# Modulation rounds interleaved with an RWKV recurrence in program order

## The chip, the cores and the metric

The kernel runs on one core of one Trainium2 chip. The metric is the device time of one execution in microseconds (us). Before the change it is 2808.48 us, the median of 3 runs (2804.44 to 2815.34). Times below are counted from the start of the profiled span.

## The reference

Two transformer blocks of depth 2 run one after the other on 256 tokens of width 1024 (a context of 256 tokens goes with them). Layer 0 of the first block mixes tokens with an RWKV-7 recurrence and a Mamba scan; the other three layers are neighbourhood attention with experts, differential attention with a short convolution, and a Fourier mixer. Each of the four layers is steered by a *modulation*: six vectors of 1024 (shift, scale and gate, twice), computed from a conditioning vector alone:

```python
m_lat = jnp.split((c_lat_act @ w_ada[i] + b_ada[i])[:, None, :], 6, axis=-1)
a_lat = _modulate(_rms_norm(h_lat, norm_mix[i]), m_lat[0], m_lat[1])
...
def step(S, inp):
    r_t, w_t, k_t, v_t, a_t, b_t = inp
    sa = jnp.einsum('bhvk,bhk->bhv', S, a_t)
    S = S * w_t[:, :, None, :] + sa[..., None] * b_t[:, :, None, :] + v_t[..., None] * k_t[:, :, None, :]
    return S, jnp.einsum('bhvk,bhk->bhv', S, r_t)
```

Everything is in 32-bit floats. The weights of the four modulations are 4 x 1024 x 6144 numbers, some 100 MB.

## The kernel before

**The modulations in rounds.** Each layer's modulation is cut into 3 rounds, 12 in all (`ADA`). A round (`ada_round`, L360) reads 8 slices of 128 rows by 2048 columns, each as two loads of 512 KB into `raw` tiles on SyncE's queue (`ada_load`, L345 to L353), and issues 4 matmuls per slice (L377) into the one bank `ada`. The four write 32 partitions each. Then VectorE adds the bias into `adar` (L380), ScalarE's queue stores it to `mrows` (L383), TensorE transposes it into `adat` (L386), and VectorE copies the columns to `mcol` (L391). Five `raw` buffers serve the rounds here, and the layer weights before and after them. `filler(n)` (L396) advances the rounds by n pieces; a round has 10 pieces.

**The recurrence.** Round 0 is done before anything else. The other 11 rounds stand beside the recurrence (`rwkv`, L798), which handles 8 blocks (2 halves of the tokens, 2 sub-blocks, 2 groups of heads). For each block k, P prepares it (`lw`, `ic`, `ci`, `sc`, `et`, `bt` on TensorE; `rw_decay`, `rw_keys`, `rw_scores`), I inverts a 32x32 triangle in 31 dependent pairs of VectorE instructions (L1012, L1013), Q completes the inverse (`m`), and C runs the two chunk steps (`rw_step`, L1048): products into `Z`, copies to `zs` and `UV` on ScalarE and VectorE, products again, and the new state `YM` (L1095). The blocks' triangles go through device memory: `dsc` to `E` before the inverse (L765, L768) and `dx` to `EA` after it (L1018, L1022), half of each on SyncE's queue, between the loads of the rounds. F (`rw_finish`, L1105) normalises a finished half (L1114 to L1122), transposes it (`yT`), multiplies with the gate (`gt`) and writes `rkv` (L1144). The sequence of these parts is a written list:

```python
ORDER = 'P0 I0 P1 I1 Q0 C0 P2 I2 Q1 C1 P3 I3 Q2 C2 F0 P4 I4 Q3 C3 F1 P5 I5 Q4 C4 P6 I6 Q5 C5 P7 I7 Q6 C6 F2 Q7 C7 F3'
```

After F3, `rw_end` (L831) splits the mixer's output in two float32r parts, `oH` and `oL`. `mixer_out` (L1369) loads the residual rows `h` on ScalarE's queue (L506), and the output projection begins: its weights are split into `wh` on ScalarE (L203) and `wl` on VectorE (L204), and its products go to `xs` (L248 to L250).

**What sets the order.** The Tile framework orders each engine's instructions by simulating the program: of what is ready, the instruction with the highest priority goes first, and priority falls with the place in the program. In this kernel all 11 rounds stand in the program ahead of the recurrence, but with their priority lowered by 100000, so that anything of the recurrence that is ready goes first. On the chip each engine then runs its list strictly in that order.

Of the kernel before, what the change touches and what calls it, by code (L numbers as in the profile page):

```python
# [51 lines left out]
HOT = 0  # L52
WB = 1, 1
HOTM = 100000
APRI = -100000
NROW = 5
NU, ND, NM, NYM, NB, NR, NW, NMB = 8, 3, 4, 6, 2, 6, 4, 7
NFIRST = 3000
# [7 lines left out]
class Builder:  # L66
# [221 lines left out]
    def weave(s, *gens, fill=0):  # L288

        gens = [[g, n] for g, n in gens]  # L290
        while gens:
            for x in list(gens):
                for _ in range(x[1]):
                    if next(x[0], s_end) is s_end:
                        gens.remove(x)
                        break
                while fill and s.work >= fill:
                    s.work -= fill
                    s.filler(1)


    def pool(s, name, bufs, **kw):
# [348 lines left out]
    def in_proj(s, xH, xL):  # L651
        nc, I = s.nc, s.I
        W = I["mix_w_in"]
        z13, t0, t1 = s.misc
        s.tl = [t0, t1]

        def ev(j, p):
            if j == 0:
                z12 = s.row(nm="z12")
                s.shift_mix(12, p, z12)  # L660
                for d in range(2):
                    for o in (32, 96):
                        nc.gpsimd.memset(s.tl[d][o:o + 1, :], 1.0)
                    nc.scalar.activation(s.tl[d][0:32, :], z12[32 * d:32 * d + 32, :], AF.Tanh)
                    nc.vector.tensor_copy(s.tl[d][64:96, :], z12[64 + 32 * d:96 + 32 * d, :])
            else:
                s.shift_mix(13, p, z13)

                nc.scalar.activation(z13[0:96, :], z13[0:96, :], AF.Tanh, scale=0.5)
                nc.gpsimd.tensor_scalar(z13[0:96, :], z13[0:96, :], 0.5, 0.5, op0=ALU.mult, op1=ALU.add)  # L670
        s.run(s.wstat2(I["wi_misc"], xH, xL, ev))
        s.z13 = z13
        s.rkv = {}
        s.rw_init()

        def krv_proj(half):
            for nm, o in (("k", 512), ("r", 0), ("v", 1024)):
                if nm == "k":
                    for th in range(2):
                        s.KR[th, half] = s.unit(nm="KR").rearrange("p (x j t) -> p x j t", x=2, j=2)  # L680
                if nm == "v":
                    t = s.rkv["v", half] = s.mx.tile([128, 2, 512], F32, name=s.n("rkv"))
                    z = lambda j: t[:, j]
                else:
                    z = lambda j: [s.KR[th, half][:, int(nm == "r"), j] for th in range(2)]
                yield from s.wstat2(W[:, o + half * 256:o + half * 256 + 256], xH, xL,
                                    lambda j, p: s.shift_mix(o // 128 + half * 2 + j, p, z(j)))
                if nm == "k":
                    s.rw_kk(half)

        s.xbc = [s.unit(nm="xbc").rearrange("p (a t) -> p a t", a=2) for _ in range(4)]
        s.xbc = [x[:, a] for x in s.xbc for a in range(2)]
        s.dump("@xbc")
        for c in range(4):
            s.run(s.wstat2(W[:, 2272 + c * 256:2272 + c * 256 + 256], xH, xL,
                           lambda j, p: s.conv5(c * 2 + j, p, s.xbc[c * 2 + j])))

        s.zg = [s.unit(nm="zg").rearrange("p (a t) -> p a t", a=2) for _ in range(2)]
        s.zg = [x[:, a] for x in s.zg for a in range(2)]

        def z_proj():
            yield from s.xstat(W, slice(1760, 2272), xH, xL, range(4), lambda t, p: nc.scalar.activation(s.zg[t], p, AF.Silu))
        s.dump("@weave")
        s.weave((s.hot(s.mamba(), HOTM), WB[0]), (s.chain(krv_proj(0), z_proj(), krv_proj(1)), WB[1]))
        xH = xL = None
        s.wstop()
        s.dump("@ada")
        s.fill = ADA[1:NADA]
        with s.tc.high_priority(offset=APRI):
            s.filler(999)  # L710
        s.run(s.rwkv())
        s.dump("@s7")
        s.rw_end()

# [1645 lines left out]
```

## Time and profile before

| | |
|---|---|
| median of 3 runs | 2808.48 us |
| the profiled execution | 2815.26 us |
| its span (first to last instruction) | 2813.5 us |
| mean granted TensorE clock | 0.945 |
| the recurrence with its 11 rounds | about 246 to 688 us |
| busy shares | TensorE 93%, VectorE 67%, ScalarE 46%, GpSimd 6% |

The profile's "busy" is the union of an engine's instructions; TensorE's weight loads (PEld) are counted apart. An engine that waits at the head of its list shows as idle, with the instruction or transfer that ended the wait. The fp32 matmuls leave two records each, so the 4 matmuls of a slice are 8 records and a round is 64. The granted clock is a mean between 0.5 (1.2 GHz) and 1.0 (2.4 GHz).

### The profile page before, as it was taken

Reading aid. Unit: us, or ns where it says so; the run is one execution under the profiler, and the core shown is the slowest. Engines: PE = TensorE matmul, PEld = TensorE weight load, DVE = VectorE, ACT = ScalarE, POOL = GpSimd, SP = SyncE. Lnnn points to the kernel's source line nnn. Section 1 sums busy time; section 2 is a strip of 40 time slices with the busy share of each in tenths; the row PEclk is TensorE's granted clock in tenths of the full one; section 3 lists DMA queues with packets and bytes.
Section 4 is the critical chain, followed back from the end, with each engine's and each line's share of the span. In section 5 each row is a group of like instructions: output and inputs, shape, how many; then the busy total and the mean of one; then the engine's idle time right before and its main releaser. Section 6 shows DMA issues by size and latency. Waiting matters only on the chain. (4 is left out here: it accounts for less than half of the span.)

```text
span 2813.5 us, 40633 instructions
## 1 busy us (share of the span) xinstructions
PE 2623.4 (93%) x15434; PEld 2094.0 (74%) x15434; DVE 1885.7 (67%) x3039; ACT 1287.7 (46%) x1760; POOL 171.5 (6%) x276
## 2 busy tenths in 40 slices
PE   6999899997999998999999999999998987997798
PEld 3776456553888887887788888888876866996797
DVE  4657877833634448456798988898896566555655
ACT  3532122111432223444688777777775443443343
POOL 0112222210000000000000000000000000000000
PEclk8999887887999999999899999999999998998899
DMA  6224776667433333333599999999996324653552
GB/s 238 87 75 161 271 242 195 205 212 276 136 97 98 98 91 105 85 111 112 207 369 349 343 346 344 364 362 340 359 343 238 122 92 148 189 186 99 162 183 75
DMA packets 324444, 570.83 MB, mean 203 GB/s; under 512 B 61752, under 2 KB 167608, under 8 KB 324240
## 3 DMA queue, kind: packets, MB, share of 16 engines
q1 hardware_dynamic: 304064, 544.61, 56.4%
q10 hardware_dynamic: 16784, 11.74, 1.4%
q0 software_dynamic: 3392, 11.80, 1.2%
q8 instruction: 123, 2.02, 0.3%
q14 instruction: 81, 0.66, 0.1%
HBM read 563.79 MB, written 4.28 MB: 202 GB/s over the span
## 5 line engine op out<-in xcount | busy, mean ns | idle before, releaser
L204 DVE TENSOR_TENSOR wl<-raw,wh 128x1024 fp32r<-128x1024 f32 x828 | 984.7, 1222 | 421.7 <-ACT wh L203 401.9
L203 ACT CAST wh<-raw 128x1024 fp32r<-128x1024 f32 x828 | 838.7, 1050 | 506.6 <-issue 191.7
L249 PE MATMUL ws<-xL,wh 128*128 128x256 f32 (+1 forms) x1392 | 456.3, 328 | 3.7 <-DVE xL L204 3.7
L248 PE MATMUL ws<-xH,wh 128*128 128x256 f32 (+1 forms) x1392 | 458.1, 331 | 0.8 <-DVE xTf L482 0.5
L250 PE MATMUL ws<-xH,wl 128*128 128x256 f32 (+1 forms) x1392 | 457.3, 329 | 0.9 <-DVE wl L204 0.9
L249 PE MATMUL mw<-wl,eH 128*128 128x512 f32 (+1 forms) x768 | 289.7, 377 | 1.4 <-DVE wl L204 1.2
L248 PEld LDWEIGHTS ws<-xH,wh 128*128 128x128 f32 x1392 | 265.3, 191 | 33.3 <-issue 7.8
L249 PEld LDWEIGHTS ws<-xL,wh 128*128 128x128 f32 x1392 | 265.1, 190 | 30.7 <-DVE xL L204 4.8
L248 PE MATMUL mw<-wh,eH 128*128 128x512 f32 (+1 forms) x768 | 286.1, 375 | 1.8 <-ACT wh L203 1.8
L250 PEld LDWEIGHTS ws<-xH,wl 128*128 128x128 f32 x1392 | 265.1, 190 | 29.7 <-issue 5.3
L250 PE MATMUL mw<-wh,eL 128*128 128x512 f32 (+1 forms) x768 | 286.2, 373 | 0.0
L377 PE MATMUL ada<-raw,act 128*32 128x512 f32 x768 | 175.0, 731 | 35.2 <-DMA raw<-in_w_ada 14.3
L249 PEld LDWEIGHTS mw<-wl,eH 128*128 128x128 f32 x768 | 145.0, 189 | 33.2 <-DVE wl L204 8.9
L248 PEld LDWEIGHTS mw<-wh,eH 128*128 128x128 f32 x768 | 144.9, 189 | 28.2 <-ACT wh L203 3.1
L250 PEld LDWEIGHTS mw<-wh,eL 128*128 128x128 f32 x768 | 145.0, 189 | 24.0
L249 PE MATMUL y<-wl,uH 128*128 128x512 f32 x352 | 139.6, 397 | 2.0 <-DVE wl L204 2.0
L250 PE MATMUL y<-wh,uL 128*128 128x512 f32 x352 | 135.7, 391 | 0.0
L248 PE MATMUL y<-wh,uH 128*128 128x512 f32 x352 | 115.0, 390 | 0.0
L471 PE MATMUL xT<-ident,xn 128*128 128x128 f32 x160 | 36.0, 403 | 82.8 <-DVE xn L449 51.5
L377 PEld LDWEIGHTS ada<-raw,act 128*32 128x32 f32 x768 | 28.2, 122 | 108.1 <-issue 37.7
L248 PE MATMUL o<-wh,mH 128*128 128x512 f32 x256 | 100.0, 390 | 0.0
L249 PE MATMUL o<-wl,mH 128*128 128x512 f32 x256 | 99.9, 390 | 0.0
(483 smaller groups left out, 4066.4 us busy)
## 6 DMA issues: line engine op xcount, KB each, us to landing
raw<-in_moe_w SPq DMA_DIRECT2D x528, 512.0 KB
raw<-in_mlp_w SPq DMA_DIRECT2D x128, 512.0 KB
raw<-in_w_ada SPq DMA_DIRECT2D x96, 512.0 KB
raw<-in_ada_w SPq DMA_DIRECT2D x96, 512.0 KB
raw<-in_ffn_w SPq DMA_DIRECT2D x66, 512.0 KB
raw<-in_mix_w_in SPq DMA_DIRECT2D x24, 512.0 KB
raw<-in_na_w_qkv SPq DMA_DIRECT2D x24, 512.0 KB
raw<-in_w_in SPq DMA_DIRECT2D x24, 512.0 KB
```

Of the source, the lines that this page charges most:

```text
L203: s.nc.scalar.copy(H, raw)
L204: s.nc.vector.tensor_tensor(L, raw, H, op=ALU.subtract)
L248: mm(out, lhsT=lH, rhs=rH, start=start, stop=False)
L249: mm(out, lhsT=lH, rhs=rL, start=False, stop=False)
L250: mm(out, lhsT=lL, rhs=rH, start=False, stop=stop)
L377: nc.tensor.matmul(ps[32 * j:32 * j + 32, :], lhsT=act[:, k, :], rhs=x[j // 2][:, j % 2 * 512:j % 2 * 512 + 512], start=(k == 0), stop=(k ...
L471: nc.tensor.transpose(p[:, j, t * 128:t * 128 + 128], xn[t][:, k * 128:k * 128 + 128], s.ident)
```

## The change

The 11 rounds no longer stand ahead of the recurrence at lowered priority. A new function `pace` runs the recurrence's generator; at each of its 144 yields it advances the rounds by as many of their 110 pieces as keep them level, so that they stand between the steps in the program and have the priority of that place. The constant `APRI` goes away. Matmuls, loads and copies are the same ones.

```diff
-APRI = -100000
...
+    STEPS = 8 * (5 + 3 + 2 + 7) + 4 * 2
+
+    def pace(s, gen, n):
+
+        i = 0
+        for i, _ in enumerate(gen):
+            for _ in range((i + 1) * n // s.STEPS - i * n // s.STEPS):
+                s.filler(1)
+        assert i + 1 == s.STEPS, i
+        s.filler(999)
...
         s.fill = ADA[1:NADA]
-        with s.tc.high_priority(offset=APRI):
-            s.filler(999)
-        s.run(s.rwkv())
+        s.pace(s.rwkv(), 10 * len(s.fill))
```

The scheduler makes a new list for each engine out of this. Three places of TensorE's list follow; a row `ada<-raw ... x2` is half a slice, two matmuls. Line numbers of helpers are one lower after the change, those of the rounds eleven higher, those of the recurrence nine higher.

First, the end of the recurrence. `Z_5824` and `Z_5801` are the last chunk step's products, `gt` and `yT` belong to F2 and F3, `xs` is the output projection. Before:

```order
L274 MATMUL Z_5824<-UV_3585,S_5326 128x64
L274 MATMUL Z_5824<-YM_5744,AR_5296 64x64
L377 MATMUL ada_2619<-raw_2662,act_90 32x512 x2
L274 MATMUL gt_5675<-misc_301,lora 128x256 x2
L377 MATMUL ada_2619<-raw_2663,act_90 32x512 x2
L386 MATMUL adat_2688<-ident,adar_2617 128x128 x4
L377 MATMUL ada_2699<-raw_2670,act_90 32x512 x2
L377 MATMUL ada_2699<-raw_2671,act_90 32x512 x2
L377 MATMUL ada_2699<-raw_2678,act_90 32x512 x2
L377 MATMUL ada_2699<-raw_2679,act_90 32x512 x2
```

After:

```order
L273 MATMUL Z_5801<-UV_2925,S_5160 128x64
L273 MATMUL Z_5801<-YM_5697,AR_5122 64x64
L273 MATMUL gt_5603<-misc_301,lora 128x256 x2
L273 MATMUL yT_5858<-ident,Y_4942 64x64 x16
L273 MATMUL gt_5879<-misc_301,lora 128x256 x2
L247 MATMUL xs_5958<-wh_5962,oH_5893 128x512
```

Before, 36 of the 352 matmuls of the rounds and two transposes `adat` stand behind the last `Z` (ten `ada` rows of two, of which six are shown, then F3's `yT` and `gt`, then eight more). After the change none does: the last round's transpose stands between two products of `Z_5801`.

Second, the completion of block 6's inverse (`m_5474`, `m_5475` before; `m_5347`, `m_5348` after). Before:

```order
L278 MATMUL bt_5397<-ident,bk_5303 128x128 x4
L274 MATMUL m_5475<-EA_4884,X_4982 32x32 x12
L377 MATMUL ada_2540<-raw_2519,act_90 32x512
L377 MATMUL ada_2540<-raw_2520,act_90 32x512 x2
L377 MATMUL ada_2540<-raw_2541,act_90 32x512 x2
L377 MATMUL ada_2540<-raw_2542,act_90 32x512 x2
L377 MATMUL ada_2540<-raw_2549,act_90 32x512 x2
L274 MATMUL Z_5745<-YM_5217,AR_5296 64x64 x2
```

After:

```order
L273 MATMUL m_5347<-ident,EA_4606 32x32 x10
L273 MATMUL m_5348<-EA_4606,X_4720 32x32
L388 MATMUL ada_5269<-raw_5271,act_90 32x512 x2
L388 MATMUL ada_5269<-raw_5294,act_90 32x512 x2
L388 MATMUL ada_5269<-raw_5295,act_90 32x512 x2
L388 MATMUL ada_5269<-raw_5318,act_90 32x512 x2
L388 MATMUL ada_5269<-raw_5319,act_90 32x512 x2
L273 MATMUL m_5348<-EA_4606,X_4720 32x32 x15
L388 MATMUL ada_5269<-raw_5407,act_90 32x512 x2
L273 MATMUL m_5347<-EA_4606,X_4720 32x32 x16
```

At this place 293 of the 384 matmuls of all 12 rounds stand ahead before, 340 after (counted to the last `m_5475` and `m_5348`).

Third, where block 6's preparation begins (`lw_4885` before, `lw_4607` after). Before:

```order
L278 MATMUL bt_4631<-ident,bk_4543 128x128 x4
L274 MATMUL lw_4885<-lora,misc_302 128x256
L274 MATMUL lw_4885<-lora,misc_303 128x256
L377 MATMUL ada_2380<-raw_2381,act_90 32x512 x2
L274 MATMUL Z_4409<-zs_307,EA_3689 64x64 x2
```

After:

```order
L388 MATMUL ada_4118<-raw_4323,act_90 32x512 x2
L388 MATMUL ada_4118<-raw_4324,act_90 32x512 x2
L273 MATMUL lw_4607<-lora,misc_302 128x256
L273 MATMUL ic_4608<-misc_302,lora 128x128 x2
L397 MATMUL adat_4494<-ident,adar_4116 128x128 x4
```

It stands 24 matmuls of the rounds and 108 others later than before. Over the whole recurrence, the share of its own matmuls that stands ahead of the end of each of the 11 rounds goes from 0.07, 0.10, 0.17, 0.28, 0.38, 0.49, 0.64, 0.77, 0.89, 0.99 and 1.00 to 0.06, 0.09, 0.15, 0.26, 0.38, 0.49, 0.60, 0.75, 0.82, 0.88 and 0.98.

## Rows read from the trace of the kernel before

**Rows 1.** The page: busy time of each engine

```profile
PE 2623.4 (93%) x15434; PEld 2094.0 (74%) x15434; DVE 1885.7 (67%) x3039; ACT 1287.7 (46%) x1760; POOL 171.5 (6%) x276
```

**Rows 2.** Windows: length, then busy time (and records) of each engine, clock, DMA share, GB/s

```profile
350.00:650.00 300.00, 286.05 (x2874) 175.41 (x2874) 191.14 (x637) 53.54 (x117) 65.76 (x116) 0.82 0.64 210
...
500.00:550.00 50.00, 47.54 (x588) 31.16 (x586) 37.68 (x136) 11.47 (x25) 11.97 (x23) 0.90 0.64 212
...
600.00:650.00 50.00, 49.69 (x444) 28.93 (x444) 14.49 (x38) 4.12 (x10) 9.25 (x12) 0.78 0.62 209
650.00:700.00 50.00, 34.46 (x156) 15.35 (x156) 18.04 (x38) 9.61 (x11) 2.75 (x4) 0.78 0.86 304
```

**Rows 3.** Timeline of TensorE at the end of the recurrence: start, us, instructions, idle before

```profile
645.75 0.47 PE L274 MATMUL Z<-YM,AR 64*64 64x64 f32 x2
...
654.86 4.47 PE L377 MATMUL ada<-raw,act 128*32 128x512 f32 x20 [1.48 <-issue]
661.63 4.66 PE L377 MATMUL ada<-raw,act 128*32 128x512 f32 x12 [2.30 <-DMA raw<-in_ada_w]
666.22 1.15 PE L274 MATMUL yT<-ident,Y 64*64 64x64 f32 x32
667.30 1.13 PE L274 MATMUL gt<-misc,lora 96*128 96x256 f32 x4
...
675.83 3.16 PE L377 MATMUL ada<-raw,act 128*32 128x512 f32 x8 [0.58 <-DMA raw<-in_ada_w]
679.84 0.66 PE L386 MATMUL adat<-ident,adar 128*128 128x128 f32 x4 [0.85 <-DVE adar L380]
687.93 0.76 PE L248 MATMUL xs<-wh,oH 128*128 128x512 f32 x1 [7.44 <-ACT wh L203]
```

**Rows 4.** Timelines of GpSimd, VectorE and ScalarE over the same stretch: F3 and after

```profile
647.10 1.51 POOL L1103 TENSOR_TENSOR Y<-Y,YM 64x256 f32<-64x256 f32 x2 [10.74 <-DVE YM L1095]
...
646.33 0.69 DVE L1095 TENSOR_TENSOR YM<-Z,YM 128x512 f32<-128x512 f32 x1 [4.66 <-PE Z L274]
...
652.59 0.68 DVE L1114 TENSOR_REDUCE sm<-Y 128x8 f32<-128x512 f32 x1
...
659.19 1.23 DVE L204 TENSOR_TENSOR oL<-oT,oH 128x1024 fp32r<-128x1024 f32 x1 [1.17 <-ACT oH L203]
...
661.52 0.69 DVE L1122 TENSOR_TENSOR Y<-Y,sm 128x512 f32<-128x512 f32 x1
...
669.99 1.04 ACT L203 CAST oH<-rkv 128x1024 fp32r<-128x1024 f32 x1 [1.55 <-DVE rkv L1144]
679.81 0.53 ACTq L383 DMA_DIRECT2D mrows<-adar  x1
684.54 0.84 ACTq L506 DMA_DIRECT2D h<-in_ctx  x2
...
686.79 4.83 ACT L203 CAST wh<-raw 128x1024 fp32r<-128x1024 f32 x5 [15.75 <-issue]
```

**Rows 5.** Windows of the instructions of tile ada on TensorE alone: us, busy (records), clock, DMA

```profile
550.00:650.00 100.00, 35.34 (x136) 0.80 0.63 213
250.00:300.00 50.00, 19.43 (x96) 1.00 0.74 269
646.20:687.90 41.70, 20.87 (x72) 0.75 0.75 253
```

**Rows 6.** Waits of SyncE's queue, 350 to 650 us: total us, times, longest

```profile
SPq L353 <- PE ada L377: 145.2, 61, 10.0
```

**Rows 7.** Waits of TensorE, 350 to 650 us: total us, times, longest

```profile
PE ada L377 <- DMA raw<-in_ada_w: 7.6, 8, 1.7
PE m L274 <- DMA EA<-dx: 0.9, 1, 0.9
```

**Rows 8.** One window of 10 us inside the recurrence, columns as in rows 2

```profile
470.00:480.00 10.00, 10.00 (x102) 6.40 (x103) 5.32 (x18) 1.04 (x3) 3.44 (x4) 0.61 0.18 52
```

**Rows 9.** Timeline of TensorE: the transpose that ends round 7

```profile
519.49 0.90 PE L386 MATMUL adat<-ident,adar 128*128 128x128 f32 x3
```

## The prediction

> **What bounds the kernel now.** I read the page first, for the engine that is busy: TensorE, 93% of the span [rows 1]. Then the windows, for the stretch that the change touches: from 350 to 650 us TensorE is busy 286.05 of 300 us, VectorE 191.14, and the transfers use 0.64 of their engines [rows 2]. Then TensorE's own waits in it: what is left goes mostly to loads of the rounds that are late, 7.6 us for eight of them, and hardly anything of the recurrence lets TensorE wait, 0.9 us for a transfer of the inverse [rows 7]. So in this stretch the recurrence and the rounds share one engine that is nearly full. SyncE's queue shows the other side: its loads stood 145.2 us for a `raw` buffer that TensorE had still to empty [rows 6]. The rounds go as fast as TensorE takes them, not as fast as memory could give them.
>
> The end of the stretch is different. The last product of the recurrence begins at 645.75 us and the output projection at 687.93 [rows 3]. In these 41.7 us (from 646.2) TensorE computes 72 records of the rounds, 20.87 us [rows 5], with gaps in which it waits for their loads (2.30 us at 661.63) [rows 3]. Behind the last round come its transpose at 679.84 [rows 3], the store to `mrows` at 679.81, then the loads of `h` at 684.54, which ScalarE's queue only lets go 4.7 us after that store, and only then the first weight split at 686.79 [rows 4].
>
> **The tail, taken away.** The changed list has no round behind the last product. What remains there is F3 and the start of the projection. I add it from the rows of before, each piece without what waited for rounds. From the last product's end (646.2) to GpSimd's end (648.61): 2.4 us. VectorE's and ScalarE's part of F3, 652.59 to 662.21: 9.6 [rows 4]. From `yT` at 666.22 [rows 3] to the end of the cast of `oH` at 671.03: 4.8. From the issue of the `h` loads to the first split, 684.54 to 686.79: 2.25, and to the projection's first matmul, 687.93: 1.1 [rows 3, 4]. That is 20.2 us in place of 41.7: **21.5 us less**. Bounds: if the loads of `h` wait 4.7 us again, 25 us remain; a split of 1.23 us at 659.19 lies within the 9.6 [rows 4] and may slip behind, which leaves 19. I take 20.2, since the store that `h` waited for now comes before F3 begins.
>
> **The same matmuls, put in front.** The 36 matmuls (72 records, 9 slices) and two transposes are now ahead of the last product. From 550 to 650 us 136 records cost 35.34 us, 0.26 each [rows 5]: 72 x 0.26 = 18.7 us, and two transposes of 0.66 [rows 3], 1.3: **20.0 us more**, if TensorE is full. Bounds for a record: 0.20 at the granted clock of 1.00 (19.43 us for 96), 0.29 in the tail itself (20.87 for 72) [rows 5], so 14.6 to 20.9 us for all. I take 0.26, the price in the stretch they are moved into.
>
> What they may fill is TensorE's idle time, 300 - 286.05 = 13.95 us from 350 to 650 [rows 2]. Nothing of it, or all of it, are the bounds. I take a quarter, **3.5 us less**: most of the moved work goes into the last part, and from 600 to 650 us only 0.31 us are idle [rows 2].
>
> **What else moves.** With each of the two rounds go a bias addition, four copies, a memset on GpSimd and a store on ScalarE's queue; they run beside TensorE on engines that are busy 64%, 22% and 18% of the stretch [rows 2], and cost nothing as long as TensorE is the full one. If not, the some 2 us of VectorE come into the chain. The 18 loads of the nine slices are now ahead on SyncE's queue. Behind a load that waits for a buffer (10.0 us at the longest) [rows 6] stand `dsc`, `E`, `dx` and `EA` of a later block, and behind these the inverse and its `m` on TensorE; before, that order is no better, and the waits it left were 0.9 us [rows 7]. Block 6's preparation stands 24 matmuls of rounds later, by 0.26 a record 12.5 us, and its inverse 47, some 24 us. This is the work of the rounds themselves, counted already; what it takes of the block's slack is in the rivals. The removed constant and the Python loop cost nothing on the chip.
>
> One rule is weighed here against a row. From 470 to 480 us TensorE is busy 10.00 of 10 us and is granted 0.61 of its clock, between its levels of 1.2 and 2.4 GHz [rows 8]. The Trainium skill, page "TensorE: Matmul & The Clock Gate", section "HAM oscillation — how this bites in real kernels", says that it is gaps between matmuls that bring the clock down. By that rule rounds that fill gaps would raise it; in these rows it is down without a gap, so I leave it out of the sum.
>
> **The sum.** -21.5 + 20.0 - 3.5 = -5.0 us. The profiled execution took 2815.3 us, so it would be 2810.3; against the median of 2808.5, 6.8 lower, **2803.5 us**. A measurement of this kernel tells about 0.5%, 14 us, from no change; the forecast lies within.
>
> **The rivals.**
> *The rounds fit into waits.* If the recurrence is held by its dependent steps and TensorE only looks full because rounds stand in its waits, the moved ones take all the idle time: -21.5 + 20.0 - 13.95 = -15.5, and with the cheap record (14.6 + 1.3) -19.6: about **2791 us**. For it: the steps are short and dependent, and a product that waits behind a round shows no idle time. Against: 0.31 us idle in the last 50.
>
> *The clock rises.* If fewer gaps brought the mean clock of 350 to 650 us from 0.82 to the 0.90 of 500 to 550 [rows 2], these 300 us would shrink by 300 x (1 - 0.82/0.90) = 26.7: **2777 us**. Against it stand rows 8. It is what the rule of the skill above would give.
>
> *The transfers bound it, and nothing is won.* The rounds end when their loads have come, and the recurrence, with its products behind them in the list, ends by as much later as the tail is shorter: **2808.5 us**. For it: the ends of the first six rounds have hardly moved in the new list, so the even spacing is not much of a new spacing, and the change does less than it says.
>
> *Late loads hold the recurrence: slower.* In the tail TensorE ran the rounds at the pace of their loads: 64 records from 654.86 to 678.99 us, less 2.1 us for `yT` and `gt` [rows 3], 0.344 each, 0.084 above 0.26. Before, nothing critical stood behind them. In the new list the last four rounds are packed between 0.60 and 0.98 of the recurrence, and every `Z` and `m` behind a late load waits with it. If these 256 records go at the tail's pace, 21.5 us come on top: +16.5, **2825 us**. It decides once the loads come more slowly than the list takes them: four rounds are 33.6 MB, which before took 160 us (519.49 to 679.84) [rows 3, 9], 210 GB/s, and would have to come in some 150, about 220. For it: there are waits for loads already [rows 7]. Against: 304 GB/s moved from 650 to 700 us [rows 2]. Block 6 adds to this rival: with its preparation later, its inverse may no longer be done when its turn comes.
>
> **How the numbers follow.** Forecast 0.47; rounds in waits 0.15; clock 0.08; transfers bound 0.13; late loads 0.17. The range goes from 2788 us (the cheap record and all idle time filled, 2808.5 - 19.6, rounded) to 2825 (the late loads); it leaves out the clock and a worse case of the loads, under 2 in 10. Faster by over 0.5%: the waits and the clock, 0.23. Slower: the late loads, 0.17. Within: the rest, 0.60.
>
> **What would show it.** Right: no `ada` record behind the last `Z`; that `Z` some 16 us later, near 662 us; the first `xs` matmul some 20 us behind it, near 683; TensorE busy over 95% up to there; all after it shifted alike. The tail is wrong if `xs` waits over 25 us for `h`, a split or F3. The price is wrong if the last `Z` comes before 655 (waits filled) or after 670 (late loads, with TensorE's waits for `raw` well above the 7.6 us of rows 7, or for `EA<-dx`). The forecast falls if the difference arises after 700 us, where nothing was changed.

## The result and the profile after

The changed kernel takes **2849.97 us** (median of four executions, 2844.08 to 2854.88) where the kernel before takes 2806.46 (2802.32 to 2815.34): a ratio of 1.0146, 95% interval 1.0122 to 1.017. It is slower by some 43 us; the forecast was 2803.5 us and a range up to 2825. The profiled execution took 2848.68 us, close to the median; the profiled one of the kernel before, 2815.26, was among its slowest, so that in the two traces the kernels lie 33 us apart, not 43.

The page's row of busy times and the windows of the changed kernel, in the columns of [rows 1, 2]:

```profile
PE 2651.4 (93%) x15434; PEld 2102.0 (74%) x15434; DVE 1885.9 (66%) x3039; ACT 1287.3 (45%) x1760; POOL 173.1 (6%) x276
```

```profile
350.00:650.00 300.00, 279.56 (x2523) 156.56 (x2519) 182.41 (x622) 49.47 (x107) 59.10 (x105) 0.79 0.64 210
```

TensorE has as many instructions as before and is busy 28 us more. In 300 us from 350 us on it is less busy than in [rows 2] (279.56 against 286.05) and runs 2523 records instead of 2874, at a lower granted clock (0.79 against 0.82).

TensorE's timeline at the end, against [rows 3]:

```profile
698.68 0.47 PE L273 MATMUL Z<-YM,AR 64*64 64x64 f32 x2
...
710.90 1.97 PE L273 MATMUL yT<-ident,Y 64*64 64x64 f32 x32 [9.75 <-DVE Y L1131]
...
719.32 2.07 PE L247 MATMUL xs<-wh,oH 128*128 128x512 f32 x4 [4.45 <-ACT wh L202]
```

and ScalarE's, against [rows 4]:

```profile
692.67 0.53 ACTq L394 DMA_DIRECT2D mrows<-adar  x1
...
715.87 0.85 ACTq L517 DMA_DIRECT2D h<-in_ctx  x2
...
718.22 4.83 ACT L202 CAST wh<-raw 128x1024 fp32r<-128x1024 f32 x5 [1.54 <-issue]
```

The two halves of my sum can be read here. **The tail came out as forecast**: no round stands behind the last `Z`, and from its end (698.68 + 0.47 = 699.15) to the first `xs` at 719.32 it is 20.2 us, the number that I had added up, in place of 41.7. The last store to `mrows` (692.67) now comes before F3, and the loads of `h` (715.87) no longer stand behind it. **The recurrence did not**: its last `Z` ends 53 us later than before (646.2), where I had +16.5. The first `xs` is 31 us later than in [rows 3], and the span 33 us longer: nearly all of the difference is there before the projection begins.

TensorE from 200 us to the last `Z`, before and after: all of it, then the rounds' records alone (tile `ada`; columns: busy, records, clock, DMA share, GB/s).

```profile
200.00:646.20 446.20, 421.75 (x3904) 0.86 0.63 212
...
200.00:646.20 446.20, 138.36 (x634) 0.86 0.63 212
```

```profile
200.00:699.20 499.20, 468.45 (x3990) 0.84 0.62 209
...
550.00:650.00 100.00, 36.01 (x148) 0.82 0.66 220
...
200.00:699.20 499.20, 175.28 (x704) 0.84 0.62 209
```

The 53 us, taken apart: 70 more records at the old mean of 138.36 / 634 = 0.218 us, 15.3; the price of all 704 up to 0.249, 21.7; everything else on TensorE dearer by 9.8 (293.2 against 283.4); idle time 30.75 instead of 24.45, 6.3. The price in the place they were moved into is the one I took (36.01 / 148 = 0.24 where rows 5 had 0.26). What I had not counted is that **all the work became dearer and the waits longer**.

TensorE's own waits and SyncE's queue, 350 to 650 us, against [rows 7] and [rows 6]. The first row is of the kernel before; [rows 7] left it out, the loads for the rounds of the first block:

```profile
PE ada L377 <- DMA raw<-in_w_ada: 4.4, 4, 2.7
...
PE ada L388 <- DMA raw<-in_ada_w: 10.2, 8, 2.9
...
PE m L273 <- DMA EA<-dx: 0.4, 1, 0.4
```

```profile
SPq L364 <- PE ada L388: 113.1, 56, 10.0
```

Waits for loads are 10.2 us in place of 7.6 + 4.4 = 12.0; from 200 us to the last `Z` they are 17.9 in place of 17.1. That is not the 21.5 of the rival on late loads, and `EA<-dx` costs 0.4. The 6.3 us of added idle time are thus nearly all other waits, most of them of the recurrence (12.9 us, before 7.4). SyncE's loads stood 113.1 us for a buffer, before 145.2.

**A measure for sorting the kernels.** Span times mean granted clock counts the clock that TensorE was granted over the span, its waits included, as time at the full clock (2.4 GHz). Between kernels it differs by more than between executions of one. Within one it is hardly steadier than the time: in 31 executions of the kernel before it goes from 2654 to 2671 us, and the time from 2795.70 to 2816.82. A split by it is bookkeeping: a wait for a load at a low clock counts as clock, too. Medians of all executions:

| kernel | us | clock | span x clock, us |
|---|---|---|---|
| before (31 executions) | 2806.7 | 0.949 | 2663 |
| changed (4) | 2850.0 | 0.939 | 2675 |
| e1 whole slices | 2850.0 | 0.931 | 2651 |
| e2 late blocks early | 2844.0 | 0.941 | 2675 |
| e3 priority alone | 2838.1 | 0.9455 | 2682 |
| e4 one slice (one execution) | 2778.6 | 0.914 | 2538 |
| e5 change doubled | 2882.1 | 0.9555 | 2751 |
| e6 before doubled | 2909.4 | 0.946 | 2752 |
| e7 before, whole slices | 2865.3 | 0.923 | 2646 |
| e8, e9 bites of 8, of 4 | 2839.0, 2849.6 | 0.9415, 0.9395 | 2673, 2676 |
| e10 rounds first | 2865.7 | 0.9405 | 2694 |
| e11 preparation ahead | 2855.8 | 0.942 | 2689 |
| e12 chain ahead | 2821.4 | 0.945 | 2666 |
| e13 all steps ahead | 2818.4 | 0.947 | 2665 |
| e14 last rounds in front | 2815.4 | 0.9475 | 2668 |
| e15 half of them | 2812.2 | 0.949 | 2667 |

By this bookkeeping, of the 43 us (2675 - 2663) / 0.944 = 13 are work and waits, and 2669 x (1 / 0.939 - 1 / 0.949) = 30 go with the lower clock. It does not tell what lowered the clock, nor that the 30 us would come back with it.

### The profile page after: what moved, and what is told of

It reads as the page before. It is cut to its first block, busy times and chain, and to the rows that moved or that the text cites. A ratio compares the mean times of both kernels' runs of the same rounds, so it can differ in the third digit from the quotient of the medians.

```text
span 2846.9 us, 40636 instructions
## 1 busy us (share of the span) xinstructions
PE 2651.4 (93%) x15434; PEld 2102.0 (74%) x15434; DVE 1885.9 (66%) x3039; ACT 1287.3 (45%) x1760; POOL 173.1 (6%) x276
## 5 line engine op out<-in xcount | busy, mean ns | idle before, releaser
L388 PE MATMUL ada<-raw,act 128*32 128x512 f32 x768 | 192.0, 738 | 29.7 <-DMA raw<-in_ada_w 13.1
L249 PE MATMUL o<-wh,mL 128*128 128x512 f32 x256 | 98.6, 389 | 0.0
```

What stands on the lines that cost most here:

```text
L249: mm(out, lhsT=lL, rhs=rH, start=False, stop=stop)
L388: nc.tensor.matmul(ps[32 * j:32 * j + 32, :], lhsT=act[:, k, :], rhs=x[j // 2][:, j % 2 * 512:j % 2 * 512 + 512], start=(k == 0), stop=(k ...
```

## The experiments

Theories, in the order in which they came. **A / W**: TensorE's work decides, and the new list cuts the rounds into dearer pieces (in the recurrence's stretch of TensorE's list 105 groups of rounds' matmuls, before 77). **B**: block 6's preparation is late and the last chains wait for it; its first product `lw` comes at 523 us, before at 480, and everything from there to the last `Z` takes about as long as before (176 us and 166). **C / D / S**: the rounds hold TensorE's clock up, and the change lowers it. **P**: the evenness itself does that. **G**: rounds at the priority of their place come ahead of products of the chain (generator `C`) that sets the end.

One thing needs no run: with its pieces at the same places but at the old offset of -100000, the changed program has the TensorE list of the kernel before, row for row. It is the priority that acts, not the place alone.

**e1, whole slices.** A half slice (4 records) that stands alone costs as much as a whole one (8); TensorE's timeline of the kernel before, at a granted clock of 1.00:

```profile
272.31 1.06 PE L377 MATMUL ada<-raw,act 128*32 128x512 f32 x8
274.39 1.05 PE L377 MATMUL ada<-raw,act 128*32 128x512 f32 x4
```

```diff
-            for j in range(4):
+            for j in (2, 3, 0, 1):
                 nc.tensor.matmul(ps[32 * j:32 * j + 32, :], lhsT=act[:, k, :], rhs=x[j // 2][:, j % 2 * 512:j % 2 * 512 + 512],
```

> The changed kernel, with the four matmuls of a slice in the order 2, 3, 0, 1, so that the first of them waits for the slice's second load and the list hardly holds half slices: 79 groups of rounds' matmuls between the recurrence's instead of 105, all 384 still in front of the last product, block 6's decay product behind 1769 other matmuls (1751 in the changed kernel, 1645 before). Theory A (a half slice that stands alone costs TensorE as much as a whole one, 1.05 us for 4 records against 1.06 for 8, and the change cuts the rounds into more pieces): the price of an ada record falls from 0.249 us to about 0.22, 704 x 0.03 = 21 us less, last Z near 678, about 2828 us (2815 to 2835). Theory B (block 6's and 7's preparation starts 42 us later, and the last two chains with it): block 6 stands as late as in the changed kernel, so 2850 us, within 7.

Measured: 2850.03 us, ratio to before 1.0151 (1.0107 to 1.0195). All of TensorE, then `ada`, to its last `Z`:

```profile
200.00:703.10 503.10, 450.96 (x4000) 0.80 0.63 208
...
200.00:703.10 503.10, 135.93 (x704) 0.80 0.63 208
```

The price did fall, to 0.193 us a record, 39 us in all, and **nothing was won**: the clock fell to 0.80, the other products became dearer by 22 us (315 against 293), the idle time grew by 21. Theory A has its price right; the time that it forecast (2815 to 2835) did not come, since this edit moved the clock as well.

**e2 to e4.** In e2 the generators of the named steps run at a raised priority; in e3 one number of the kernel before changes; e4 keeps one slice of eight (and its loads).

```diff
-            yield from {"P": P, "I": I, "Q": Q, "C": C, "F": F}[o[0]](int(o[1]))
+            g = {"P": P, "I": I, "Q": Q, "C": C, "F": F}[o[0]](int(o[1]))
+            yield from s.hot(g, 1000) if o in ("P6", "I6", "P7", "I7") else g
```

> The changed kernel, with the preparation and the inverse of blocks 6 and 7 at a raised priority: block 6's decay product behind 1673 other matmuls (1751 in the changed kernel, 1645 before), block 7's behind 1874 (2004; 1932 before); the list is the same up to block 5, 108 groups of rounds' matmuls (105), 14 of 384 behind the last product. Theory B: the excess of some 36 us over my forecast goes, about 2814 us (2800 to 2825). Theory A: as many pieces, the same price, 2850 us (2840 to 2858).

```diff
-APRI = -100000
+APRI = -1000
```

> The kernel before, its rounds still put ahead of the recurrence in the program, with their priority's offset -1000 instead of -100000: no even spacing, but all 384 matmuls of the rounds in front of the last product as in the changed kernel, 106 groups (77 before, 105 changed), block 6's decay product behind 1679 other matmuls (1645 before, 1751 changed). Theory A: pieces as small as in the changed kernel, 2845 us (2835 to 2855). Theory B: block 6 in time, so my forecast of step 1 comes true, 2803 us (2795 to 2815).

```diff
-        for k in range(8):
+        for k in range(1):
...
-                                 start=(k == 0), stop=(k == 7), tile_position=(0, 32 * j))
+                                 start=(k == 0), stop=(k == 0), tile_position=(0, 32 * j))
```

> The kernel before with one of eight slices of each round (seven eighths of the rounds' matmuls and loads are left out): what the recurrence takes by itself. If TensorE's work is what bounds it (theory A), 283 us of its own matmuls from 200 us on, some 16 for what is left of the rounds and some 25 idle put the last Z near 525 us, and the time near 2670 us. If the recurrence is bound by its own dependent steps (theory B needs this at least at its end), the last Z stays beyond 600 us, and the time above 2730.

Measured: e2 2843.99 us, 1.0127 (1.0095 to 1.0159); block 6's `lw` at 501 us instead of 523, and 6 us gained of the 36 that theory B wanted: not told from nothing, and within theory A's range (2840 to 2858). e3 2838.09 us, 1.0113 (1.0075 to 1.0152): a raised priority without any spacing costs two thirds of it, again in theory A's range (2835 to 2855) and far from B's 2803. e4 2778.64 us in one execution, the last `Z` at 634, only 12 us earlier than before with seven eighths of the rounds gone. Why, the windows of TensorE show (350 us to the last `Z`; no `ada` record falls in it):

```profile
350.00:634.40 284.40, 252.46 (x2260) 0.52 0.10 22
```

**Without the rounds TensorE is granted 0.52 of its clock**, all but its lower level of 1.2 GHz, although it is recorded busy 252.46 of 284.40 us. From 200 us on the rounds' records take 17 us instead of 138, and the recurrence's own products 360 instead of 283: of 121 us given up by the rounds 77 go back into these products, and 32 into idle time (56.9 us, before 24.5). By its expectation, a last `Z` beyond 600 us says that the recurrence is held by its own dependent steps; with the clock down as well, this run cannot tell the two apart. The loads are gone along with the matmuls, so the next runs change the matmuls alone.

**e5, e6, e7: the rounds doubled, and whole slices before.** `s.zero` is a tile of zeros.

```diff
-            for j in range(4):
-                nc.tensor.matmul(ps[32 * j:32 * j + 32, :], lhsT=act[:, k, :], rhs=x[j // 2][:, j % 2 * 512:j % 2 * 512 + 512],
...
+            for j in range(8):
+                jj = j % 4
+                nc.tensor.matmul(ps[32 * jj:32 * jj + 32, :], lhsT=act[:, k, :] if j < 4 else s.zero, rhs=x[jj // 2][:, jj % 2 * 512:jj % 2 * 512 + 512],
...
```

> The changed kernel, with every slice's four matmuls of the rounds issued twice, the second time with weights of zero, which adds nothing to the result: twice the rounds' dense work (512 columns) between the same steps of the recurrence. Over the whole span, span times mean granted clock is 2675 us in each of the changed kernel's executions and 2661 in the kernel's before, while the clock itself differs: 0.94 against 0.948. Added are 88 times four matmuls, 0.85 us each time at the full clock, 75 us. Theory W (the clock is given and the work counts): 2750 / 0.94, about 2925 us. Theory D (the rounds' dense matmuls hold TensorE's clock up between the recurrence's small ones, and the change slows the kernel mostly by a lower clock): the granted clock from 350 us to the last Z rises from 0.78 to over 0.9, that of the span to 0.975 or more, 2750 / 0.975, about 2820 us (2790 to 2850), so not slower than the changed kernel in spite of the added work.

> The kernel before with the same doubling; of its 768 matmuls of the rounds 206 stand behind the last Z (before 36 of 384). Theory W: (2661 + 75) / 0.948, about 2886 us. Theory D: the clock of the span rises to 0.97 or more, 2736 / 0.975, about 2806 us (2780 to 2830), as fast as before.

e7 is the edit of e1 in the kernel before.

> The kernel before with the slice's matmuls in the order 2, 3, 0, 1, hence few half slices: 65 groups of the rounds instead of 77, but 68 of 384 matmuls behind the last Z instead of 36. Theory W: the rounds cost TensorE some 30 us less in the recurrence, the longer tail takes 36 x 2 x 0.29 = 21 us back: 2800 us (2790 to 2810). Theory D: less dense work, so a lower clock there (below 0.80 from 350 us to the last Z, 0.83 before): span times clock falls to 2650 or less, the clock to 0.94 or less, and nothing is won, 2820 us (2808 to 2835).

Measured: e5 2882.14 us, 1.0265 (1.0226 to 1.0303); e6 2909.36, 1.0372 (1.0331 to 1.0413); e7 2865.34, 1.0216 (1.0176 to 1.0256). TensorE from 350 us to the last `Z`, of the changed kernel, e5, e6 and e7:

```profile
350.00:699.20 349.20, 325.87 (x2931) 0.78 0.62 206
...
350.00:736.50 386.50, 371.31 (x3651) 0.90 0.63 204
...
350.00:687.60 337.60, 321.50 (x3180) 0.80 0.48 152
...
350.00:669.80 319.80, 299.07 (x2922) 0.72 0.56 183
```

In e5 span times clock is 2751 us where 2750 was expected, and the clock rises from 0.78 to 0.90 in the stretch: of 76 us added, 32 show. D has the direction right, W and D are both wrong in size. **e6 speaks against D**: from 200 us to the last `Z` its rounds leave 1000 records instead of 634 and take 172.59 us instead of 138.36, and the clock there is 0.86 as before (0.80 from 350 us on, before 0.83). More of the rounds' work does not raise the clock by itself. The other 206 of its 768 matmuls stand behind the last `Z`.

In e7 span times clock falls by 17 us and the kernel before becomes 60 us slower. The bookkeeping puts all of it down to the clock (0.949 to 0.923); the trace does not. The last `Z` ends 23 us later, and from there to the first `xs` at 734.90 it is 65 us instead of 42, since 68 matmuls of the rounds stand there instead of 36 and TensorE runs them at the pace of their loads. TensorE to the last `Z`, its rounds in it, and the rounds behind it:

```profile
200.00:669.80 469.80, 437.03 (x3848) 0.77 0.56 185
...
200.00:669.80 469.80, 116.40 (x572) 0.77 0.56 185
...
669.80:734.90 65.10, 30.00 (x136) 0.58 0.83 284
```

In the recurrence the rounds cost 22 us less and its own products 37 us more (320.6 against 283.4), as in e1: with whole slices the rounds become cheaper, the clock falls, and the products beside them become dearer.

**e8, e9, e10: the pace.**

```diff
-            for _ in range((i + 1) * n // s.STEPS - i * n // s.STEPS):
-                s.filler(1)
+            if i % 8 == 7:
+                s.filler((i + 1) * n // s.STEPS - (i + 1 - 8) * n // s.STEPS)
```

e9 does the same at every fourth step.

> The changed kernel, with the same mean pace in coarser bites: every eighth step of the recurrence is followed by what eight steps were followed by. Of 384 matmuls of the rounds 4 stand behind the last Z, 105 groups as in the changed kernel, block 6's decay product at the same place (behind 1751 others). Theory P (the evenness of the spacing is what lowers the clock): the clock of the span is back at 0.948, 2675 / 0.948, about 2822 us. Theory S (the clock in the recurrence follows how much time the rounds' dense matmuls stream there, wherever they stand): as much streaming, so 0.939 within 0.003, span times clock 2675 within 10, about 2850 us (2838 to 2860).

> The same with bites of four steps (100 groups, 4 matmuls behind the last Z, block 6's decay product behind 1735 others): how far lists that are all but alike differ among themselves. Theory P: half of the way back at most, 2835 us. Theory S: 0.939 within 0.003, 2850 us (2838 to 2860). If e8 and e9 differ by more than 0.004 in the clock, neither holds, and the clock depends on the small order of a list.

In e10 each `s.filler(1)` of `pace` stands in `with s.tc.high_priority(offset=3000):`.

> The changed kernel, with the rounds' pieces at the same places but at a priority raised by 3000, so that they are placed as soon as their loads allow: 132 groups, and only 32 of 384 matmuls of the rounds left when block 7's decay product comes. Theory S: while the rounds last the clock is above the changed kernel's (from 350 to 550 us 0.78 there), 0.85 or more, and once they have run out it falls towards the 0.5 of the run with one slice; span times clock rises by the smaller pieces to about 2690, the time to about 2855 us (2840 to 2880). Theory P: denser rounds and no even spacing, a clock of 0.948, 2690 / 0.948, 2838 us, with no fall at the end.

Measured: e8 2839.01 us, 1.0117 (1.0086 to 1.0148), e9 2849.62, 1.0137 (1.0101 to 1.0173), e10 2865.71, 1.021 (1.018 to 1.0239). The bite of the pace moves the clock by 0.0025 at most: P falls. e10 shows inside one kernel how the clock stands with rounds and without; its last round ends before 625 us (TensorE's windows):

```profile
350.00:550.00 200.00, 190.03 (x1740) 0.88 0.73 243
550.00:625.00 75.00, 75.00 (x727) 0.92 0.70 230
...
627.00:649.00 22.00, 22.00 (x177) 0.50 0.22 55
...
630.00:700.00 70.00, 57.76 (x567) 0.50 0.11 25
```

While rounds last the clock is about 0.9; once they have run out it is 0.50, first of all in 22 us in which TensorE is recorded busy without a gap.

**e11 to e13: which steps go ahead of the rounds.** The edit of e2, with `if o[0] in "PI"` (e11), `if o[0] == "C"` (e12) and `if o[0] in "PIC"` (e13).

> The changed kernel, with the preparation and the inverse of every block at a priority raised by 1000, ahead of the rounds of their place: 316 matmuls of the rounds in front of the last Z and 36 behind it, the split of the kernel before; block 6's decay product behind 1637 others (1645 before, 1751 changed). If a late preparation is what costs (theory B): 2808 us, as before (2800 to 2815). Theory S: with a recurrence as short as before and 117 half-slice streams in it instead of 104, a clock of 0.95, but more cycles for the pieces, 2672 / 0.95, 2813 us (2805 to 2825). If neither: 2840 us and more.

> The changed kernel, with the chain's products alone (Z and what is in its generator) at a priority raised by 1000, ahead of the rounds of their place; all 384 matmuls of the rounds still in front of the last Z, 86 groups (105 changed, 77 before), block 6's decay product behind 1785 others, later than in the changed kernel. Theory G (a piece at its place's priority stands in front of chain products that are ready, and stretches the chain that sets the end): 2815 us (2805 to 2830). Theory S (cycles and the clock, by how long the rounds stream): as in the changed kernel, 2850 us (2838 to 2860). Theory B (late preparation): later than changed, 2855 us or more.

> The same with preparation, inverse and chain raised: rounds only where none of them is ready; 22 of 384 matmuls of the rounds behind the last Z, 89 groups, block 6's decay product behind 1645 others, as before. Theories G and B: 2810 us (2800 to 2822), as before. If it stays over 2835 us, neither place explains the kernel before, and its list is better in another way.

Measured: e11 2855.79 us, 1.0163 (1.0128 to 1.0198); e12 **2821.41**, 1.0047 (1.003 to 1.0064); e13 2818.42, 1.0048 (1.0019 to 1.0077). In e11 block 6's `lw` is nearly in time (493 us) and the kernel as slow as the changed one; in e12 it is late (509 us), and two thirds of the loss are gone. **B falls on both sides.** S, in its ranges for e8 to e10, misses twice: it had 2813 us for e11 and 2850 for e12. **G has the time of e12 right** (2805 to 2830); whether it has the reason, the trace must say. TensorE of e12, all of it and the rounds, against the same rows of before and after above:

```profile
200.00:678.10 478.10, 445.07 (x3988) 0.87 0.65 218
...
200.00:678.10 478.10, 156.20 (x704) 0.87 0.65 218
```

The stretch is 21 us shorter than in the changed kernel. Of these, 19 lie in the rounds' own records (156.20 against 175.28), 4 in the other products (288.9 against 293.2), and TensorE idles 2 us more (33.0). Span times clock is back to 2666 and the clock of the span to 0.945; by the bookkeeping above, 10 us of the 29 gained are work and waits, 18 the clock.

So G's reason is not shown, and a rival stands beside it, theory A once more. Raising the chain also changed how the rounds are cut: 86 groups of their matmuls instead of 105 (e13: 89). Among the kernels that leave the order in a slice alone, the time goes with that number: 77 to 91 groups (before, e12 to e15) take 2807 to 2821 us, 100 to 108 (changed, e2, e3, e8, e9, e11 with 107) 2838 to 2856, and 132 (e10) 2866. Whole slices break the rule, at a lower clock: e1 has 79 and takes 2850, e7 has 65 and takes 2865. Nor does the standing of the chain sort the kernels. Worked out from the waits written in each program and the semaphore times in its trace, the `Z` products that wait for a copy stood ready behind rounds for some 86 us in all before, 101 in the changed kernel, 95 in e12 and 52 in e10, the slowest of the four. No run raises the chain and keeps 105 groups.

What a wait behind rounds looks like in the changed kernel: TensorE at the end of block 6's inverse, for which the chain waits (generator `Q`, whose priority none of these runs changes).

```profile
626.75 0.24 PE L273 MATMUL m<-EA,X 32*32 32x32 f32 x2 [0.45 <-DMA EA<-dx]
626.92 1.05 PE L388 MATMUL ada<-raw,act 128*32 128x512 f32 x4
630.65 1.05 PE L388 MATMUL ada<-raw,act 128*32 128x512 f32 x4 [2.68 <-DMA raw<-in_ada_w]
631.89 4.41 PE L388 MATMUL ada<-raw,act 128*32 128x512 f32 x12 [0.19 <-DMA raw<-in_ada_w]
636.23 0.69 PE L273 MATMUL m<-EA,X 32*32 32x32 f32 x30
...
639.90 0.32 PE L273 MATMUL Z<-zs,EA 64*64 64x64 f32 x2
```

The first of 16 small products runs at 626.75, the other 15 at 636.23, behind 20 records of the rounds and 2.9 us of waiting for their loads; the chain's `Z` comes only then. How much earlier the other 15 could have run these rows do not say. It is one place, and with it the rival on late loads is real in small.

**e14, e15: my forecast alone.** The list of the kernel before up to block 7, and only the last rounds moved.

```diff
         with s.tc.high_priority(offset=APRI):
-            s.filler(999)
+            s.filler(80)
+        with s.tc.high_priority(offset=-1000):
+            s.filler(999)
```

> The kernel before, with the last 30 of its 110 pieces at an offset of -1000: TensorE's list is that of the kernel before up to block 7's decay product (270 matmuls of the rounds, 1932 others ahead of it, as before), and only the last three rounds move in front of the last Z; 91 groups. It is my forecast's edit without a new list for the rest. If my sum holds (21.5 us off the tail, 20 for the matmuls moved), with some 8 us for finer pieces: 2811 us (2800 to 2822). If rounds in front of the last chains cost what they do in the changed kernel: 2840 us or more, the last Z beyond 680.

In e15, 90 stands for 80.

> The same with the last 20 pieces: 14 of 384 matmuls of the rounds stay behind the last Z, 86 groups. My sum: 2809 us (2800 to 2820). Otherwise between before and the run with 30 pieces, 2825 us.

Measured: e14 2815.36 us, 1.0029 (1.0009 to 1.0049); e15 2812.23, 1.0008 (0.9988 to 1.0028). This is what I had summed up: the tail's gain and the moved matmuls nearly cancel. My sum had -5 us and e14 shows +9. TensorE of e14 to its last `Z`, all of it and the rounds:

```profile
200.00:673.80 473.80, 442.95 (x3993) 0.88 0.66 221
...
200.00:673.80 473.80, 161.57 (x704) 0.88 0.66 221
```

Against before, 70 more records at the old price are 15.3 us, the price of all 704 (0.229 for 0.218, with 91 groups for 77) 7.9, idle time 6.4 and the other products -2.0. No version that does all of the work beats the kernel before.

## Why the prediction was wrong

- **The tail**: right, 20.2 us.
- **The same matmuls in front**: right as a price in the new place, and e14, which does only this, ends at +9 us where my sum had -5. It is off by the finer pieces, half slices that cost as much as whole ones, of which I had counted none (7.9 us in e14), and by idle time (6.4 us more in e14).
- **Idle time filled, -3.5 us**: wrong in sign; 6.3 us more of it, nearly all of it not for loads.
- **The step that failed** is "Block 6's preparation stands 24 matmuls of rounds later [...] This is the work of the rounds themselves, counted already". I had taken the moves of the other nine rounds as neutral, since the same work stands in the list, and counted only the two that change sides. In place of that nothing, the changed kernel pays 21.7 us in the price of all 704 records (0.218 to 0.249) and 9.8 us in the recurrence's own products. The list of before with the last rounds alone moved loses 9 us (e14), the whole new list 43, and with only the chain raised above the rounds 15 (e12). So it is the order of the whole list, made by rounds at the priority of their place, that costs. By which way stays open: the finer pieces, the chain behind the rounds, and the clock that goes with either are not told apart. Block 6, which I named in that sentence, is late as I said, and it does not matter (e11, e12).
- **The clock**: I left it out of the sum by [rows 8], down to 0.61 without a gap, and had a rival only for a rise. By the bookkeeping, 30 of the 43 us go with it. The rows were right and my use of them wrong: a clock that is down without a gap says that something other than gaps holds it, and I should have asked what. Rounds left out give 0.52 (e4), rounds used up 0.50 (e10), rounds doubled 0.90 in the changed kernel (e5) and no more than before in the kernel before (e6). The Trainium skill, page "TensorE: Matmul & The Clock Gate", section "HAM oscillation — how this bites in real kernels", explains a low clock by gaps between matmuls; in e10 TensorE is recorded busy for 22.00 of 22 us at 0.50, and in e4 for 89% of the stretch at 0.52, so the rule alone does not carry this case.
- **The rival that came closest**, late loads (2825 us), had the right side and another mechanism: up to the last `Z` the waits for `raw` grew by 0.8 us.
- **What stays open**: why the new list is dearer, by finer pieces or by the chain's place, and why the clock is higher when the chain goes first (0.945 against 0.939, with the same rounds in front of the last `Z`). That the clock falls to its lower level where the rounds are missing is shown (e4, e10); that more of them raise it is not, since e5 and e6 differ. The doubled matmuls carried zeros, and no run was made with others.

## What to carry to other kernels

Work that fills TensorE beside a dependent chain did best here below that chain in priority (before, e12, e13); at the priority of its place it made a dearer list, even where the amount of work in front of the end was the same. Where such work is cut into pieces, count them: here a half piece cost as much as a whole one. Before costing TensorE's work by its records, look at the granted clock: here cheaper rounds (e1, e7) came with a lower clock and dearer products beside them, and nothing was won. An edit that moves a few instructions in a scheduled list is priced by the whole new list, and a run that moves only those instructions (e14) tells the two apart.

## What was not expected of the hardware

A record of TensorE being busy does not mean that its clock stays up: 22.00 of 22 us busy at 0.50 in e10, once the rounds had run out, and 75.00 of 75 at 0.92 just before. And half of a slice (two matmuls, 4 records) took 1.05 us at the full clock, a whole slice (four, 8 records) 1.06.
